# Two-layer hybrid encoder in float32: scheduling the state-space stage with shared and larger PSUM tiles, ScalarE order edges and sixteen filler projections

## Chip, cores and metric

The kernel runs on one core of a Trainium2 chip. The metric is the device time of one execution in microseconds. A TensorE weight load and the product that uses it are two instructions; the profile calls the first PEld and the second PE.

## The reference

A sequence of 1024 tokens of width 1024 goes through two layers, all in float32. Layer 0 multiplies by one wide matrix and splits the result: `z`, the state-space input `xbc` (x, B and C), `dt`, and four branches `Bg, Cg, h, gate` of a short convolution. Cut to what matters here:

```python
xbc = silu(depthwise_conv(xbc, conv_w) + conv_b)
cb = einsum('bclgn,bcsgn->bcgls', cq, bq)                      # C.B of a chunk of 128 tokens
y_diag = einsum('bcgls,bcgrls,bcsgrp->bclgrp', cb, segsum_exp(cs), xd)
states = einsum('bclgn,bcgrl,bclgrp->bcgrpn', bq, decay_states, xd)
y_off = einsum('bclgn,bcgrpn,bcgrl->bclgrp', cq, h_in, exp(cs))
y_a = rms_norm((y_diag + y_off) * silu(z))                     # both directions summed
y_b = sc_bg * depthwise_conv(sc_cg * sc_h) * silu(sc_gate)
x = layer_norm(alpha * x + concat([y_a, y_b]) @ w_out)
```

There are 4 groups of 4 heads and 8 chunks, in two directions. Layer 1 is an attention with rotary keys beside a pooling branch; its cosine and sine tables depend on the positions alone.

## The kernel before, in words

Every large product keeps float32 accuracy by splitting both operands into a high and a low part in the `fp32r` type (`split`, L492: a ScalarE cast, then a subtraction on VectorE or GpSimd) and adding three products (`mm3`, `mm6`).

Layer 0 (`layer0_main`, L501) goes in stages. First come `z` of group 0 and `dt`, accumulated in PSUM tiles `zdp` that `op_zx` (L568) empties. Then four branch tiles of 128 columns; each is a **filler**: 8 steps of `op_fm` (L678), 6 products a step, 48 products of 512 columns in a tile `gps`. Beside them `op_tp` (L853) loads x again, subtracts its quarters on VectorE and splits them into the four tiles `xT`, the right-hand sides of a Strassen scheme. `op_sw` and `op_sp` (L867, L923) then do two projection tiles as a **pair** in 84 products instead of 96: the eight pairs of B, C and x in front, and the pairs of the branches not yet done at the back.

Between the two lies the **state-space stage**, group by group. For each chunk `op_p2` (L721) transposes x and B (tile `xps`), multiplies by the decay (`xd` on VectorE) and splits it (`xdh` by a ScalarE cast, `xdl` on GpSimd); `op_p2s` (L741) multiplies to the chunk's state (`sps`), and the states are chained in `hin`. For groups 1 to 3 `op_z` (L701) computes that group's z in the same loop, 24 products of 256 columns in `zps`, with a tanh on ScalarE and a product on VectorE into the tile `zx`. Then, for each chunk, `op_p3f` (L780) multiplies C.B (`cbp`), loads a row of sums into all partitions (`E`, 512 KB), and makes the decay matrix: four biased copies on ScalarE (L794), a mask copied to PSUM (L795), a predicated copy on VectorE (L796), four exponentials (L798) and the product with C.B (L803). `op_p3b` (L808) adds the off-diagonal output `yo`, the diagonal output `yd` (four products with the decay matrix, L823) and the skip term, multiplies by z on GpSimd (L830) and squares on ScalarE (L831). `op_end` (L834) turns the sums of squares into `rinv`, which TensorE transposes (L841).

Fillers from a queue are laid between these steps by `main_plan` (L77): `FX` steps before group 0, `F2[g]` at each chunk of the first loop, `F3[g]` at each of the second. `J0` says how many branch columns of 128 are fillers; the rest are pairs. Within a plan step the Tile scheduler orders the instructions of each engine by its own timing, but it keeps an order that `tc.issue_after` gives: instructions of the block stand behind the one named, on that one's engine. `op_hold` (L674) uses this to keep fillers from being drawn ahead of a group's last transpose.

PSUM has two pools: `pa`, two tiles of 1024 columns (two banks each), and `pb`, four of one bank. Before, `gps` lies in `pa`; `xps`, `sps`, `zps`, `cbp`, `yo` and `yd` take turns in `pb`. The rotary tables (`rope_tables`, L351) are computed in group 2.

```python
F2, F3, FB, FX = (1, 0, 0, 0), (3, 2, 2, 3), 0, 8
JF, J0 = 1, 4
with tc.issue_after(st["xd", C2[E_AT]]):    # a VectorE instruction; L794 to L796 are in the block
```

Of the kernel before, what the change touches and what calls it, by code (L numbers as in the profile page):

```python
# [9 lines left out]
F32 = mybir.dt.float32  # L10
# [53 lines left out]
F2, F3, FB, FX = (1, 0, 0, 0), (3, 2, 2, 3), 0, 8  # L64
JF, J0 = 1, 4
# [3 lines left out]
ROPE_AT = (2, 2)  # L69
# [7 lines left out]
def main_plan():  # L77
# [41 lines left out]
    for g in range(G):  # L119
        ops.append(("z0", g))  # L120
        pull(FB)
        for i, c in enumerate(C2):
            ops.append(("p2", g, c))
            if g > 0:
                ops.append(("z", g, c))
            pull(F2[g])
            if (g, i) == ROPE_AT:
                ops.append(("rope",))
            if i > 0:
                ops.append(("p2s", g, C2[i - 1]))  # L130
# [15 lines left out]
        ops.append(("hold", None))  # L146
# [6 lines left out]
    pull(len(queue))  # L153
    ops.append(("sw", NF + 1, 0))
# [337 lines left out]
def split(nc, hi, lo, src, lo_eng, scale=None):  # L492
    if scale is None:
        nc.scalar.copy(out=hi, in_=src)  # L494
        lo_eng.tensor_tensor(out=lo, in0=src, in1=hi.bitcast(F32), op=ALU.subtract)  # L495
    else:
        nc.scalar.mul(out=hi, in_=src, mul=scale)
        nc.vector.scalar_tensor_tensor(out=lo, in0=src, scalar=scale, in1=hi.bitcast(F32), op0=ALU.mult, op1=ALU.subtract)


def layer0_main(k):  # L501
# [66 lines left out]
    def op_zx():  # L568
# [3 lines left out]
        for c, n, p in [(0, 2, zpair[0]), (2, 2, zpair[1])] + [(c, 1, zps[c].unsqueeze(1)) for c in range(4, NB)]:  # L572
# [4 lines left out]
            V.scalar_tensor_tensor(out=zs, in0=zt, scalar=1.0, in1=p[:, :, 0:256], op0=ALU.add, op1=ALU.mult)  # L577
# [55 lines left out]
    br = {}  # L633

# [39 lines left out]
    def op_hold(g):  # L674
        nonlocal hold
        hold = None if g is None else groups[g]["xp"]
# [24 lines left out]
    def op_z(g, c):  # L701
        st = groups[g]
        h, o = c // 4, (c % 4) * P
        ps = k.pb.tile([P, 512], F32, name="zps", tag="pb")[:, 0:256]
# [16 lines left out]
    def op_p2(g, c):  # L721
# [58 lines left out]
    def op_p3f(g, c):  # L780
# [11 lines left out]
        with tc.issue_after(st["xd", C2[E_AT]]):  # L792
# [58 lines left out]
    T = {}  # L851

    def op_tp(kk):  # L853
# [4 lines left out]
        for o, p, q in ((a0, a1, a0), (a1, b1, a1), (b1, b1, a0), (b0, b0, b1)):  # L858
            V.tensor_tensor(out=o, in0=p, in1=q, op=ALU.subtract)
# [763 lines left out]
```

## Time and profile before

| what | value |
|---|---|
| runs | 1483.84, 1486.55, 1487.31 us; median 1486.55 |
| profiled execution | 1484.99 us, its span 1483.2 us |
| granted TensorE clock, mean of the span | 0.968 |
| first stage, front pairs begin | 89.5 us |
| state-space stage, first transpose to last diagonal output | 253.8 to 601.6 us |
| first product of the back pairs | 617.7 us |
| back pairs end, output projection begins | about 773 us |

The span is the time from the first to the last instruction. An engine's busy time says how long it had an instruction in work, and not whether that ran at its best rate. The granted clock is TensorE's: 1 is 2.4 GHz, 0.5 is 1.2 GHz, and a value between is a mean over a stretch that had both.

### The profile page before, as it was taken

What the parts mean: (1) busy time and instruction counts of PE and PEld (TensorE: products, weight loads), DVE (VectorE), ACT (ScalarE), POOL (GpSimd) and SP (SyncE); (2) the same over time, 40 slices, a digit from 0 to 9 for tenths busy, and PEclk for the clock granted to TensorE, in tenths of its full rate; (3) what the DMA queues carried; (4) which work ended last, traced back from release to release, by engine and by line L of the source; (5) the groups of instructions that cost most, each with busy time, mean ns of one, the idle gap of its engine ahead of it and who ended that gap; (6) DMA issues with size and microseconds to landing.
All of it is one profiled execution on the core that took longest, in us unless ns stands there. A gap on an engine that the chain in (4) does not pass through costs nothing.

```text
span 1483.2 us, 19661 instructions
## 1 busy us (share of the span) xinstructions
PE 1394.1 (94%) x7191; PEld 1184.5 (80%) x7191; DVE 941.9 (64%) x1576; ACT 700.5 (47%) x1359; POOL 476.4 (32%) x459
## 2 busy tenths in 40 slices
PE   7999999697978899499999999999999999999997
PEld 7778888477867797388888888898888889888886
DVE  5758886364747558776656363643334888888575
ACT  4335554455554655343334342432223788888510
POOL 0022220353544545533320060242140255546311
PEclk9999999798989899799999999999999999999999
DMA  7412336544351613422236736311110000001232
GB/s 244 143 61 101 113 114 226 143 117 139 93 164 29 173 41 103 153 75 89 71 91 208 247 126 216 110 58 43 44 36 0 1 1 1 1 30 57 72 128 86
DMA packets 55520, 146.40 MB, mean 99 GB/s; under 512 B 6264, under 2 KB 11648, under 8 KB 55296
## 3 DMA queue, kind: packets, MB, share of 16 engines
q1 hardware_dynamic: 55424, 145.15, 31.4%
q8 instruction: 57, 0.93, 0.3%
q14 instruction: 39, 0.32, 0.1%
HBM read 118.78 MB, written 26.35 MB: 98 GB/s over the span
## 4 chain that ended last, share of the span: by engine, by line
PE 79%; DMA 7%; DVE 6%; ACT 3%; issue 3%; POOL 1%; SPq 0%; DVEq 0%; ACTq 0%; POOLq 0%
PE sA L939 12%; PE sD L939 6%; DMA E<-crow 5%; PE ops L423 4%; PE ops L425 4%; PE ops L422 4%; PE tps L1445 3%; PE fps L416 3%; PE sB L939 3%; PE fps L415 3%; PE fps L417 3%; PE gps L422 2%; PE gps L423 2%; PE sps L415 2%; PE gps L425 2%
## 5 line engine op out<-in xcount | busy, mean ns | idle before, releaser
L422 PE MATMUL gps<-x,whi 128*128 128x512 f32 x256 | 104.8, 409 | 6.3 <-DVE dtx L573 6.3
L1431 POOL TENSOR_SCALAR pt<-pt,sm 128x1024 f32<-128x1024 f32 x64 | 72.9, 1139 | 114.6 <-DVE sm L1430 63.8
L495 DVE TENSOR_TENSOR wlo<-wraw,whi 128x1024 fp32r<-128x1024 f32 x50 | 64.9, 1299 | 65.4 <-ACT whi L494 65.3
L423 PE MATMUL gps<-x,whi 128*128 128x512 f32 x256 | 104.8, 410 | 0.0
L888 POOL TENSOR_TENSOR s3t<-sraw 128x512 f32<-128x512 f32 x16 | 27.5, 1722 | 226.8 <-DMA sraw<-in_wt_dram 172.5
L494 ACT CAST whi<-wraw 128x1024 fp32r<-128x1024 f32 x50 | 52.3, 1049 | 94.7 <-PE ops L425 39.2
L495 DVE TENSOR_TENSOR PT<-tps,PT 128x512 fp32r<-128x512 f32 x128 | 84.2, 682 | 12.6 <-ACT PT L494 12.3
L425 PE MATMUL gps<-x,wlo 128*128 128x512 f32 x256 | 86.9, 410 | 0.0
L1425 DVE TENSOR_REDUCE nm<-sps 128x1 f32<-128x1024 f32 x64 | 78.0, 1218 | 9.2 <-PE sps L417 8.9
L1042 POOL TENSOR_TENSOR rs<-rs,neghalf 128x1 f32<-128x1 f32 x16 | 12.9, 810 | 210.5 <-DVE nm L1077 142.8
L1429 ACT ACTIVATE pt<-sps,nm 128x1024 f32<-128x1024 f32 x64 | 71.8, 1122 | 17.9 <-DVE nm L1426 15.2
L494 ACT CAST PT<-tps 128x512 fp32r<-128x512 f32 x128 | 70.0, 588 | 15.8 <-PE tps L1445 15.3
L495 POOL TENSOR_TENSOR xdl<-xd,xdh 128x512 fp32r<-128x512 f32 (+1 forms) x32 | 36.8, 1150 | 125.5 <-ACT xdh L494 115.9
L415 PE MATMUL fps<-x1hi,whi 128*128 128x512 f32 x192 | 74.9, 390 | 0.0
L417 PE MATMUL fps<-x1hi,wlo 128*128 128x512 f32 x192 | 74.7, 389 | 0.0
L416 PE MATMUL fps<-x1lo,whi 128*128 128x512 f32 x192 | 74.7, 389 | 0.0
L1445 PE MATMUL tps<-consts,pt 128*128 128x128 f32 x512 | 70.1, 272 | 0.5 <-DVE PT L495 0.5
L794 ACT ACTIVATE E<-E,ed 128x128 f32<-128x128 f32 x128 | 41.2, 390 | 57.4 <-DMA E<-crow 54.5
L629 DVE SCALAR_TENSOR_TENSOR cacc<-u,vec,cacc 128x1023 f32<-128x1023 f32 (+1 forms) x48 | 66.8, 1407 | 1.5 <-ACT cacc L626 1.3
L1460 PE MATMUL yps<-PT,vv 128*128 128x256 f32 x256 | 65.7, 286 | 0.0
L1445 PEld LDWEIGHTS tps<-consts,pt 128*128 128x128 f32 x512 | 59.7, 141 | 7.2 <-DVE PT L495 1.1
L494 ACT CAST whi<-sraw 128x1024 fp32r<-128x1024 f32 x40 | 41.2, 1049 | 50.4 <-PE sD L939 40.9
(381 smaller groups left out, 4357.7 us busy)
## 6 DMA issues: line engine op xcount, KB each, us to landing
wraw<-in_wt_dram SPq DMA_DIRECT2D x66, 512.0 KB, 4.4
sraw<-in_wt_dram SPq DMA_DIRECT2D x32, 512.0 KB, 3.6
E<-crow SPq DMA_DIRECT2D x32, 512.0 KB, 5.5
xtraw<-in_xT_dram SPq DMA_DIRECT2D x16, 512.0 KB, 4.3
xbd<-cacc SPq DMA_DIRECT2D x16, 512.0 KB, 2.6
xfm<-xbd SPq DMA_DIRECT2D x16, 512.0 KB, 6.8
ybd<-bra SPq DMA_DIRECT2D x16, 256.0 KB, 3.1
yad<-yg SPq DMA_DIRECT2D x32, 128.0 KB, 3.4
```

What stands on the lines that cost most here:

```text
L415: nc.tensor.matmul(out, shi, mhi, start=start, stop=False)
L416: nc.tensor.matmul(out, shi, mlo, start=False, stop=False)
L417: nc.tensor.matmul(out, slo, mhi, start=False, stop=stop)
L422: nc.tensor.matmul(out, shi, mhi, start=start, stop=False)
L423: nc.tensor.matmul(out, shi, mlo, start=False, stop=False)
L425: nc.tensor.matmul(out, slo, mhi, start=False, stop=stop)
L494: nc.scalar.copy(out=hi, in_=src)
L495: lo_eng.tensor_tensor(out=lo, in0=src, in1=hi.bitcast(F32), op=ALU.subtract)
L939: PE.matmul(ps, s_[:, kk, :], x_, start=fresh and kk == 0 and m == 0, stop=kk == 3 and m == 2, skip_group_check=True)
L1425: V.tensor_reduce(out=nm, in_=ps, axis=AX.X, op=ALU.max)
L1431: GP.tensor_scalar(out=pt, in0=pt, scalar1=sm, scalar2=1.0, op0=ALU.mult, op1=ALU.mult)
L1445: PE.transpose(out=ps[:, P * c:P * c + P], in_=pt[:, P * (4 * h + c):P * (4 * h + c) + P], identity=k.ident)
```

## The change

The diagonal output `yd` is put into the second half of the bank that held C.B (`cbp[:, 256:512]`), instead of a bank of its own. `zps` moves to the pool of large tiles. The biased copies and the mask copy of the decay matrix now stand behind the ScalarE cast `xdh` of the sixth chunk, where the edge before named a VectorE instruction. The subtractions of `op_tp` in front stand behind the last product of `op_zx` on VectorE. The rotary tables go to the output projection of layer 0, at its third weight. There are 16 fillers instead of 12 and six back pairs instead of eight; three fillers are held behind the last diagonal output.

```diff
-F2, F3, FB, FX = (1, 0, 0, 0), (3, 2, 2, 3), 0, 8
-JF, J0 = 1, 4
+F2, F3, FB, FX = (2, 0, 0, 0), (3, 3, 2, 2), 0, 8
+JF, J0 = 1, 5
...
-            if (g, i) == ROPE_AT:
-                ops.append(("rope",))
...
-        ops.append(("hold", None))
+        ops.append(("hold", None if g + 1 < G else "end"))
...
     pull(len(queue))
+    ops.append(("hold", None))
     ops.append(("sw", NF + 1, 0))
...
-            V.scalar_tensor_tensor(out=zs, in0=zt, scalar=1.0, in1=p[:, :, 0:256], op0=ALU.add, op1=ALU.mult)
+            T["after"] = V.scalar_tensor_tensor(out=zs, in0=zt, scalar=1.0, in1=p[:, :, 0:256], op0=ALU.add, op1=ALU.mult).ins
...
-        hold = None if g is None else groups[g]["xp"]
+        hold = None if g is None else groups[-1]["yd"] if g == "end" else groups[g]["xp"]
...
-        ps = k.pb.tile([P, 512], F32, name="zps", tag="pb")[:, 0:256]
+        ps = k.pa.tile([P, 1024], F32, name="zps", tag="pa")[:, 0:256]
...
-        split(nc, xh[:, cols], xl[:, cols], xd[:, cols], nc.gpsimd)
+        st["xa", c] = split(nc, xh[:, cols], xl[:, cols], xd[:, cols], nc.gpsimd)
...
-        with tc.issue_after(st["xd", C2[E_AT]]):
+        with tc.issue_after(st["xa", C2[E_AT]]):
...
-        st["f", c] = E
+        st["f", c] = E2[:, 0], cbp[:, 2 * P:4 * P]
...
-        yd = k.pb.tile([P, 512], F32, name="yd", tag="pb")[:, 0:256]
         for h in range(HPG):
-            PE.matmul(yd[:, HD * h:HD * h + HD], M[:, P * h:P * h + P], xt[:, HD * h:HD * h + HD], start=True, stop=True)
+            st["yd"] = PE.matmul(yd[:, HD * h:HD * h + HD], M[:, P * h:P * h + P], xt[:, HD * h:HD * h + HD], start=True, stop=True).ins
...
-        for o, p, q in ((a0, a1, a0), (a1, b1, a1), (b1, b1, a0), (b0, b0, b1)):
-            V.tensor_tensor(out=o, in0=p, in1=q, op=ALU.subtract)
+        with tc.issue_after(T["after"]) if "after" in T else nullcontext():
+            for o, p, q in ((a0, a1, a0), (a1, b1, a1), (b1, b1, a0), (b0, b0, b1)):
+                V.tensor_tensor(out=o, in0=p, in1=q, op=ALU.subtract)
...
+            if h == 0 and kk == ROPE_AT:
+                slots = [t[:, i] for t in (view(t4("rope"), 8) for _ in range(2)) for i in range(8)]
+                rope_tables(k, lambda name: slots.pop(0))
```

What the scheduler makes of it is shown at three places. The first is ScalarE in the first loop of group 0 (`xdh` the cast of a chunk's decayed x, `E` its biased copies, `zx`, `bhl` and `hin` copies out of PSUM). Before:

```order
145 L494 CAST xdh<-xd 128x256
146 L794 ACTIVATE E_2208<-E_2208,ed 128x128 x4
147 L641 ACTIVATE bra<-bru,vec 128x512 x2
148 L728 COPY zx<-xps 128x256
149 L494 CAST bhl<-xps 128x128
150 L794 ACTIVATE E_2227<-E_2227,ed 128x128 x4
151 L757 COPY hin<-sps 128x256
152 L494 CAST xdh<-xd 128x256
153 L794 ACTIVATE E_2289<-E_2289,ed 128x128 x4
154 L794 ACTIVATE E_2344<-E_2344,ed 128x128 x4
155 L494 CAST xdh<-xd 128x512
```

In the changed kernel, from the casts of the fifth and sixth chunk on:

```order
161 L493 CAST xdh<-xd 128x512 x2
162 L729 COPY zx<-xps 128x256
163 L493 CAST bhl<-xps 128x128
164 L795 ACTIVATE E_2265<-E_2265,ed 128x128 x4
165 L795 ACTIVATE E_2284<-E_2284,ed 128x128 x4
166 L795 ACTIVATE E_2345<-E_2345,ed 128x128 x4
167 L795 ACTIVATE E_2399<-E_2399,ed 128x128 x4
168 L493 CAST xdh<-xd 128x512
```

The biased copies of four chunks, which stood between the casts of the first three chunks, have moved behind the cast of the sixth.

The second place is TensorE from the end of group 0 to group 1 (`gps` a filler, `yo` and `yd` a chunk's outputs, `cbp` C.B, `xps` and `zps` transposes and z of group 1). Before:

```order
1105 L786 MATMUL cbp_2588<-xfm_1885 128x128
1106 L817 MATMUL yo_2625<-hin_1949,xfm_1885 128x256
1107 L823 MATMUL yd_2629<-zx_1947,E2_2518 128x64 x4
1108 L817 MATMUL yo_2662<-hin_1949,xfm_1885 128x256
1109 L823 MATMUL yd_2666<-zx_1947,E2_2590 128x64 x4
1110 L727 MATMUL xps_2693<-consts_63,xfm_2201 128x128 x3
1111 L415 MATMUL zps_2707<-whi_2551,x00_90 128x256
```

In the changed kernel (products on a `cbp` tile from L822 are diagonal outputs):

```order
1154 L822 MATMUL cbp_2522<-zx_1947,E2_2524 128x64 x4
1155 L424 MATMUL gps_2609<-x11_93,wlo_2439 128x512
1156 L414 MATMUL zps_2763<-whi_2603,x00_90 128x256
1157 L415 MATMUL zps_2763<-wlo_2604,x00_90 128x256
1158 L787 MATMUL cbp_2639<-xfm_1885 128x128
1159 L416 MATMUL zps_2763<-whi_2603,x00_90 128x256
1160 L414 MATMUL zps_2763<-whi_2603,x00_90 128x256
1161 L415 MATMUL zps_2763<-wlo_2604,x00_90 128x256
1162 L822 MATMUL cbp_2576<-zx_1947,E2_2578 128x64 x2
1163 L817 MATMUL yo_2676<-hin_1949,xfm_1885 128x256
```

Two tiles of z of the next group now lie between the last three diagonal outputs of the group, where nothing lay before.

The third place is TensorE at the end of the stage (`rinvp` the transpose of `rinv`, `sA` the first product of the back pairs). Before:

```order
2178 L425 MATMUL gps<-x_93,wlo 128x512
2179 L817 MATMUL yo<-hin,xfm 128x256
2180 L823 MATMUL yd<-zx,E_5187 128x64 x4
2181 L817 MATMUL yo<-hin,xfm 128x256
2182 L823 MATMUL yd<-zx,E_5245 128x64 x4
2183 L841 MATMUL rinvp<-consts,rinv 8x128
2184 L939 MATMUL sA<-x_90,whi 128x512 x2
```

In the changed kernel, around the same transpose:

```order
2286 L421 MATMUL gps<-x_90,whi 128x512
2287 L422 MATMUL gps<-x_90,whi 128x512
2288 L421 MATMUL gps<-x_92,whi 128x512
2289 L840 MATMUL rinvp<-consts,rinv 8x128
2290 L422 MATMUL gps<-x_92,whi 128x512
2291 L424 MATMUL gps<-x_90,wlo 128x512
```

Between the last diagonal output and that transpose there are now 57 filler products, and 39 more stand between it and the first product of the back pairs; the third held filler is laid into the first pair.

## Rows read from the trace of the kernel before

**Rows 1.** The page: busy time, share of the span and instructions of TensorE.

```profile
PE 1394.1 (94%) x7191; PEld 1184.5 (80%) x7191; DVE 941.9 (64%) x1576; ACT 700.5 (47%) x1359; POOL 476.4 (32%) x459
```

**Rows 2.** Stretch, length; busy PE, PEld, DVE, ACT, POOL; PEclk, DMA share, GB/s.

```profile
253.80:300.30 46.50, 33.78 (x145) 26.27 (x144) 19.29 (x32) 21.69 (x57) 13.17 (x15) 0.82 0.56 150
300.30:347.20 46.90, 39.10 (x194) 31.00 (x193) 30.03 (x69) 28.68 (x87) 27.56 (x36) 0.93 0.54 143
347.20:383.60 36.40, 36.35 (x259) 34.54 (x259) 15.09 (x35) 17.88 (x49) 14.63 (x16) 0.94 0.26 88
383.60:427.00 43.40, 37.16 (x176) 29.16 (x174) 31.93 (x70) 24.45 (x79) 23.31 (x35) 0.88 0.54 137
427.00:472.90 45.90, 39.88 (x260) 36.52 (x261) 27.55 (x78) 22.19 (x59) 15.50 (x17) 0.89 0.27 79
472.90:514.60 41.70, 36.66 (x175) 29.07 (x174) 28.31 (x64) 25.01 (x80) 25.17 (x35) 0.88 0.54 150
514.60:551.60 37.00, 36.65 (x260) 34.61 (x260) 15.15 (x35) 19.25 (x55) 16.20 (x19) 0.95 0.19 45
551.60:601.60 50.00, 45.48 (x223) 36.05 (x221) 43.03 (x84) 26.13 (x77) 25.31 (x32) 0.99 0.41 114
601.60:617.60 16.00, 0.03 (x1) 0.06 (x1) 11.45 (x15) 4.37 (x9) 11.25 (x10) 0.50 0.57 179
...
617.60:772.70 155.10, 155.10 (x694) 128.30 (x694) 99.19 (x105) 56.59 (x77) 48.36 (x32) 0.99 0.27 85
```

**Rows 3.** The chain that ended last, front pairs: start, duration, what.

```profile
150.04 2.73 PE sA L939 x12
...
169.19 2.73 PE sA L939 x12
```

**Rows 4.** Timeline of TensorE in group 0's second loop: start, duration, what.

```profile
320.92 1.02 PE L817 MATMUL yo<-hin,xfm 128*128 128x512 f32 x2
321.38 0.80 PE L422 MATMUL gps<-x,whi 128*128 128x512 f32 x1
...
322.72 1.00 PE L823 MATMUL yd<-zx,E 128*128 128x64 f32 x8
323.55 0.44 PE L786 MATMUL cbp<-xfm 128*128 128x128 f32 x2
323.75 0.48 PE L425 MATMUL gps<-x,wlo 128*128 128x512 f32 x1
```

**Rows 5.** Timeline of TensorE, two transposes of group 1, one chunk apart.

```profile
363.49 0.49 PE L727 MATMUL xps<-consts,xfm 128*128 128x128 f32 x3
...
367.38 0.49 PE L727 MATMUL xps<-consts,xfm 128*128 128x128 f32 x3
```

**Rows 6.** The chain that ended last, one product of z in group 1.

```profile
357.38 0.12 PE zps L416
```

**Rows 7.** What TensorE waited for from 250 to 620: total, times, longest.

```profile
PE sps L415 <- ACT xdh L494: 16.2, 5, 6.0
...
PE yd L823 <- DVE E L803: 3.2, 3, 1.6
```

**Rows 8.** Groups by line: ScalarE's biased copies, busy, mean ns, idle before and releaser.

```profile
L794 ACT ACTIVATE E<-E,ed 128x128 f32<-128x128 f32 x128 | 41.2, 390 | 57.4 <-DMA E<-crow 54.5 <-PE yd L823 3.0
```

**Rows 9.** Timeline of TensorE, diagonal outputs at the end of group 1.

```profile
421.22 1.94 PE L823 MATMUL yd<-zx,E 128*128 128x64 f32 x8 [2.92 <-issue]
...
425.23 1.97 PE L823 MATMUL yd<-zx,E 128*128 128x64 f32 x8 [1.11 <-DVE E L803]
```

**Rows 10.** Timeline of VectorE and TensorE in the first stage, before the first filler.

```profile
34.55 2.14 DVE L859 TENSOR_TENSOR xtraw<-xtraw 128x512 f32<-128x512 f32 x3 [1.43 <-DMA xtraw<-in_xT_dram]
...
39.34 0.68 DVE L577 SCALAR_TENSOR_TENSOR z<-zt,zdp 128x512 f32<-128x512 f32 x1
```

**Rows 11.** Timeline of TensorE in the first stage: last `zdp` product, first filler.

```profile
33.54 0.29 PE L417 MATMUL zdp<-zdh,x 128*128 128x288 f32 x1
40.17 0.77 PE L422 MATMUL gps<-x,whi 128*128 128x512 f32 x1 [6.33 <-DVE dtx L573]
```

More of the change, by code (lines that the diff above doesn't have):

```diff
@@ L68 @@
 E_AT = 5
-ROPE_AT = (2, 2)
+ROPE_AT = 2
 L1_ORDER = "t0 l2 t1 l3 t2 l4 t3 l5 m0 l6 m1 l7".split()
@@ L493, in split @@
     if scale is None:
-        nc.scalar.copy(out=hi, in_=src)
+        cast = nc.scalar.copy(out=hi, in_=src)
         lo_eng.tensor_tensor(out=lo, in0=src, in1=hi.bitcast(F32), op=ALU.subtract)
     else:
-        nc.scalar.mul(out=hi, in_=src, mul=scale)
+        cast = nc.scalar.mul(out=hi, in_=src, mul=scale)
         nc.vector.scalar_tensor_tensor(out=lo, in0=src, scalar=scale, in1=hi.bitcast(F32), op0=ALU.mult, op1=ALU.subtract)
+    return cast.ins
 def layer0_main(k):
@@ L633, in layer0_main @@
     br = {}
+    T = {}
     def br_conv(u, j):
@@ L735, in op_p2 @@
         d = dirs(cols)
-        st["xd", c] = V.tensor_tensor(out=xd.rearrange("p (q h d) -> p q h d", q=2, h=HPG)[:, d], in0=bc_mid(xv, 1, d.stop - d.start), in1=bc_last(dw4[:, c, d, g4], HD), op=ALU.mult).ins
+        V.tensor_tensor(out=xd.rearrange("p (q h d) -> p q h d", q=2, h=HPG)[:, d], in0=bc_mid(xv, 1, d.stop - d.start), in1=bc_last(dw4[:, c, d, g4], HD), op=ALU.mult)
         xh, xl = t2("xdh", F32R), t2("xdl", F32R)
-        split(nc, xh[:, cols], xl[:, cols], xd[:, cols], nc.gpsimd)
+        st["xa", c] = split(nc, xh[:, cols], xl[:, cols], xd[:, cols], nc.gpsimd)
         st["s", c] = (bh, bl, xh[:, cols], xl[:, cols])
@@ L804, in op_p3f @@
         st["cd", c] = cd[:, 0:4]
-        E = E2[:, 0]
-        st["f", c] = E
+        st["f", c] = E2[:, 0], cbp[:, 2 * P:4 * P]
     def op_p3b(g, c):
         st = groups[g]
-        M = st.pop(("f", c))
+        M, yd = st.pop(("f", c))
         g4 = slice(4 * g, 4 * g + 4)
@@ L849, in op_end @@
         nc.sync.dma_start(out=k.rrow, in_=rd.rearrange("c t -> (c t)").unsqueeze(0).partition_broadcast(P))
-    T = {}
     def op_tp(kk):
@@ L857, in op_tp @@
         a0, a1, b0, b1 = ra[:, 0:HALF], ra[:, HALF:S], rb[:, 0:HALF], rb[:, HALF:S]
-        for o, p, q in ((a0, a1, a0), (a1, b1, a1), (b1, b1, a0), (b0, b0, b1)):
-            V.tensor_tensor(out=o, in0=p, in1=q, op=ALU.subtract)
+        with tc.issue_after(T["after"]) if "after" in T else nullcontext():
+            for o, p, q in ((a0, a1, a0), (a1, b1, a1), (b1, b1, a0), (b0, b0, b1)):
+                V.tensor_tensor(out=o, in0=p, in1=q, op=ALU.subtract)
+        if kk == 3:
+            T.pop("after", None)
         t = big(k, "xT4").rearrange("p (s a t) -> p s a t", s=2, a=4)
@@ L1015, in op_ya @@
         split(nc, t[:, 0, :, o:o + P], t[:, 1, :, o:o + P], view(y, KD), V)
-    table = {"fm": op_fm, "hold": op_hold, "zx": op_zx, "ssd": op_ssd, "xl": op_xl, "z0": op_z0, "z": op_z, "p2": op_p2, "p2s": op_p2s, "p2b": op_p2b, "p3f": op_p3f, "p3b": op_p3b, "dt": op_dt, "rope": lambda: rope_tables(k, t2), "end": op_end, "ya": op_ya, "tp": op_tp, "sw": op_sw, "sp": op_sp}
+    table = {"fm": op_fm, "hold": op_hold, "zx": op_zx, "ssd": op_ssd, "xl": op_xl, "z0": op_z0, "z": op_z, "p2": op_p2, "p2s": op_p2s, "p2b": op_p2b, "p3f": op_p3f, "p3b": op_p3b, "dt": op_dt, "end": op_end, "ya": op_ya, "tp": op_tp, "sw": op_sw, "sp": op_sp}
     for op in main_plan():
```

## The prediction

> **What bounds the kernel now.** The page comes first: TensorE is busy 1394.1 of 1483.2 us, and no other engine is busy for more than two thirds of the span [rows 1]. So time can be won only where TensorE stands still or runs slowly, or by giving it fewer products. The table by stretch says where [rows 2]: in the back pairs it is busy all the time at a clock of 0.99, while in the 363.8 us from the first transpose of the state-space stage to the back pairs it is busy 305.1 and the clock is as low as 0.82.
>
> Busy is not the whole story there, since a product that runs at half clock or waits inside its slot counts as busy. So I count what each stretch would need at the pace of the trace's good places. A filler product takes 2.73 / 12 = 0.227 us [rows 3], a filler of 48 products 10.9. A chunk of the second loop takes 0.46 for `yo`, 0.83 for `yd` and 0.20 for C.B, 1.49 in all, by the starts that follow one another [rows 4]. A chunk of the first loop with z takes 367.38 - 363.49 = 3.89 [rows 5]; z alone is 24 x 0.12 = 2.9 [rows 6], so a chunk of group 0, without z, takes about 1.0. The number of filler products in each stretch is read from TensorE's order.
>
> - Group 0, first loop: 46.5 less (96 x 0.227 + 8 x 1.0 = 29.8): **16.7 lost**. Second loop: 46.9 less (96 x 0.227 + 8 x 1.49 = 33.7): **13.2**.
> - Group 1: 36.4 less (16 x 0.227 + 8 x 3.89 = 34.7): **1.7**; 43.4 less (80 x 0.227 + 11.9 = 30.1): **13.3**.
> - Group 2: 45.9 less 34.7: **11.2**; 41.7 less 30.1: **11.6**.
> - Group 3: 37.0 less 34.7: **2.3**; 50.0 less (128 x 0.227 + 11.9 = 41.0): **9.0**.
> - End, last `yd` to the back pairs: **16.0**.
>
> That is 95.0 us, of which the busy column shows 58.7 as idle. The waits say what the largest are: 16.2 us for the cast `xdh` [rows 7], 16.0 at the end where TensorE is busy for 0.03 [rows 2]. ScalarE itself stood idle for 54.5 us before its biased copies, waiting for `E` to land [rows 8]; its queue is in order, so the casts behind those copies waited too.
>
> **The change part by part.** *Order edges on ScalarE.* In group 0 the copies of four chunks stood between the casts of the first three; now they stand behind the sixth. Most of TensorE's 16.2 us for casts lay there (five waits, the longest 6.0 [rows 7]). With two filler steps a chunk instead of one the loop also has cover for the 16 copies (16 x 41.2 / 128 = 5.1 us [rows 8]) that now precede the last two casts. Bounds for what stays lost: 2 (as in group 1's first loop) and 16.7. I take 4, nearer to group 1, since the order has 30 filler products, 6.8 us, right beside those copies.
>
> *Rotary tables.* They go out of group 2's first loop, which then resembles groups 1 and 3 (1.7 and 2.3 lost): 2 instead of 11.2. VectorE was busy 27.6 us there and 15.1 in group 1's first loop [rows 2], so some 12 us go. In the output projection the order lays them singly between the weight splits, and VectorE is busy 64% over the span [rows 1]; so I cost them at 1 us, with bounds 0 and 5. The cover is the next weight, split one step ahead; if it goes, TensorE waits for that weight.
>
> *z in large tiles, shared bank.* In the tails of the second loops nothing lay between the last outputs, and TensorE went cold: `yd` took 1.94 there [rows 9] and 1.00 beside fillers [rows 4], and two outputs lay 425.23 - 421.22 = 4.0 us apart, 2.5 more than their work. Now two z of the next group, 5.8 us, lie there in groups 0 to 2. They are not new work, only earlier. But the tile `zx` that they are written to is free only when GpSimd has read the last chunk, and `pa` has two slots; so the third z waits for last `yd`, sum, product and evacuation, about 3 us, and with the cold clock after it I put 4 at each of the three boundaries (bounds 0 and 6). What is queued behind that z on TensorE are the transposes and states of group 1 to 3, so all of it is on the path.
>
> *Fillers.* Group 0 and 1 have 3 steps for each chunk, 4.1 us beside 1.49, more than the 4.0 of an unfilled chunk: 6 and 5 stay lost. Group 2 has 2, and its order has four outputs behind the last z: 4 x 2.5 = 10 if nothing had run ahead; I take 9. Group 3 has 2 where it had 3, five outputs without filler or z (5 x 2.5 = 12.5), and VectorE there still has the quarters of x to split (it was busy 43.0 of 50.0 [rows 2]): 14 instead of 9.0. At the end 57 products, 12.9 us, lie ahead of `rinvp`, which came 16.0 after the last output: about 2 stays, slow clock included. In sum the losses kept are 4 + 6 + (2 + 4) + 5 + (2 + 4) + 9 + (2 + 4) + 14 + 2 = 58 of 95: **37 won**. The work itself grows: four fillers, 43.6, against two pairs of 169.19 - 150.04 = 19.15 [rows 3], 38.3: **5.3 lost**.
>
> *First stage.* The first filler started at 40.17 after a gap of 6.33 [rows 11], because VectorE had subtractions and splits of x ahead of the product that frees the tile; that product ran at 39.34 for 0.68 [rows 10]. Behind the edge the gap needs the addition, a tanh and that product, an estimate of 1.7 us; and without the long gap the first products don't run cold. I take **5 won**, bounds 0 and 6. What is queued behind on VectorE is the split of x and, through its three raw buffers on SP's queue, the first pair's weights. They have room: the front pairs start only after four fillers, 43.6 us.
>
> Sum: 37 - 5.3 + 5 - 1 = 35.7 us. The profiled execution took 1484.99, so 1449.3, and I say **1449**; the median of the runs shown is 1486.55, 1.6 above that execution. With the bounds at their good ends (30 us kept) it would be 1419, with the bad ones (87 kept, nothing won in front, 5 lost on the tables) 1487.
>
> **The rivals.** *Everything fills.* If with more chunks in flight the decay chain runs ahead, the tails of groups 2 and 3 shrink with the others. For it: ScalarE no longer waits for `E` in line, and a chunk's copies take it 41.2 / 32 = 1.3 us [rows 8], far under 4.0. Against it: VectorE's load in group 3. With 35 kept: 60 - 5.3 + 5 = 59.7, **1425**.
>
> *The chunk's pace stays.* C.B now holds its bank until the diagonal output has been read. If that ties the next chunk as much as a third bank did, the second loops lose what they lost before (13.2, 13.3, 11.6) and group 3 some 18 with five bare chunks; with 4 + 6 + 6 + 6 for the first loops and 2 at the end that is 80 kept: 15 - 5.3 + 5 - 1 = 13.7, **1471**. For it: pace 4.0 in a tail that had all engines free. Against it: `yd` already waited for the last reading of C.B (3.2 us in three waits [rows 7]), so the sharing adds no wait of its own. The Trainium skill speaks on its side: Perfetto Trace Analysis, under Matmuls, wants independent groups of products to rotate through different PSUM banks so that emptying one overlaps the next; by that rule this change would cost what this rival costs, and no run here shows the shared bank yet.
>
> *A wait takes the place of the one removed (slower).* The biased copies now stand in the first loops, where z has only two slots. If `E` lands later than the sixth cast, ScalarE waits with the tanh of z, the last casts and copies behind it, and TensorE stops within two chunks. The wait that ScalarE had was 54.5 us [rows 8]. If all of it reached TensorE, 35.7 - 54.5 = -18.8, **1504**; it decides from 35.7 of the 54.5 on. Against it: the loads of `E` stand in SP's queue as early as before, and the copies come three chunks later.
>
> *The edge in front doesn't help.* The tiles of x come late, and the first pair waits as long as the filler did: 5 lost instead of won, **1459**.
>
> **How the numbers follow.** Forecast 0.60, everything fills 0.14, pace stays 0.14, the edge in front 0.07, slower 0.05. The forecast's own range is 1435 to 1465; to hold 8 in 10 it reaches to the first rival and to the second's edge: **1424 to 1470**. A change of 0.3%, 4.5 us, is about what a measurement can tell from none. Only the slower rival and the worst bounds of the second come near that line: faster 0.92, same 0.03, slower 0.05.
>
> **What would show it.** Right: no wait of TensorE for `xdh` above 2 us in group 0; first filler near 35.5 us; group 2's first loop near 38; two z between the last outputs with a gap of some 3 us behind them; gaps and a low clock left in the tails of groups 2 and 3; `rinvp` with a wait under 4. Wrong: gaps on TensorE for tanh or `xdh` behind the copies, outputs still 4 us apart beside fillers, waits for a weight while the rotary tables run, or front pairs that begin no earlier than 89 us.

## The result, and the profile after

The changed kernel takes 1450.68 us (median of 4 runs, 1448.25 to 1452.92), the kernel before beside it 1486.93 (1483.84 to 1488.05): a ratio of 0.976, 95% interval 0.974 to 0.978, 36 us less. The forecast was 1449. The profiled execution has a span of 1448.4 us against 1483.2, so 34.8 us less; the sum had come to 35.7. That nearness is partly luck: the term for the first stage was wrong by more than its size, and the stage made it good, as the stretches show.

The page of the changed kernel: busy time, share of the span and instructions of TensorE. TensorE is busy as long as before, in a shorter span [rows 1].

```profile
PE 1393.8 (96%) x7215; PEld 1184.6 (82%) x7215; DVE 925.5 (64%) x1564; ACT 693.6 (48%) x1350; POOL 464.8 (32%) x452
```

The same nine stretches as in [rows 2], now each second loop ending with the group's last diagonal output; the last one ends with the first product of the back pairs.

```profile
254.20:297.70 43.50, 40.86 (x189) 33.30 (x188) 22.03 (x35) 22.62 (x58) 13.31 (x15) 0.96 0.60 173
297.70:342.80 45.10, 44.99 (x251) 37.37 (x250) 34.13 (x72) 26.27 (x76) 25.72 (x34) 1.00 0.56 139
342.80:378.10 35.30, 31.92 (x216) 29.89 (x215) 15.96 (x34) 20.41 (x62) 16.12 (x19) 0.90 0.40 120
378.10:426.60 48.50, 48.50 (x266) 40.39 (x265) 30.40 (x69) 25.53 (x78) 27.40 (x38) 1.00 0.47 140
426.60:459.10 32.50, 31.70 (x223) 29.24 (x223) 14.58 (x33) 19.55 (x58) 15.55 (x16) 1.00 0.35 118
459.10:502.60 43.50, 39.97 (x214) 32.99 (x213) 30.75 (x71) 22.86 (x71) 21.75 (x31) 0.91 0.47 123
502.60:541.20 38.60, 32.74 (x215) 30.54 (x214) 16.52 (x34) 20.48 (x60) 16.30 (x18) 0.84 0.18 51
541.20:584.60 43.40, 37.77 (x169) 28.01 (x168) 35.17 (x75) 24.69 (x75) 27.55 (x34) 0.88 0.44 115
584.60:609.30 24.70, 22.21 (x98) 17.71 (x97) 17.77 (x23) 8.91 (x15) 8.03 (x8) 1.00 0.46 143
```

With the unit costs of the prediction and the products that TensorE's order has in each stretch, the losses can be set beside the ones it expected to stay. For group 0's first loop, for example, 135 filler products make 30.6 and eight chunks 8.0, so 43.5 - 38.6 = 4.9 are lost. Products of z that now run in the loop before are counted where they run.

| stretch | lost before | predicted to stay | lost after |
|---|---|---|---|
| group 0, first / second loop | 16.7 / 13.2 | 4 / 6 | 4.9 / 3.2 |
| group 1 | 1.7 / 13.3 | 6 / 5 | 5.5 / 2.8 |
| group 2 | 11.2 / 11.6 | 6 / 9 | 1.1 / 9.7 |
| group 3 | 2.3 / 9.0 | 6 / 14 | 8.8 / 14.5 |
| end | 16.0 | 2 | 2.7 |
| sum | 95.0 | 58 | 53.2 |

So 41.8 us came out of this stage's losses instead of 37. What TensorE still waits for there (its waits from 250 to 622 us: total, times, longest) is mostly the tile `zx` at the three group boundaries, which before did not show; the casts, 16.2 before [rows 7], are down to 2.6.

```profile
PE zps L414 <- DVE zx L711: 9.9, 3, 5.9
PE cbp L787 <- DVE to L820: 3.8, 2, 3.0
PE yo L817 <- DVE to L820: 3.6, 2, 2.6
PE sps L414 <- ACT xdh L493: 2.6, 1, 2.6
```

The three waits for `zx` are 3.4, 0.7 and 5.9 us. The trace names what stands behind the longest: `zx` is written at 508.66, when GpSimd has finished its last product `yg` (507.93 to 508.65). The sum which that product reads was ready at 506.20, and GpSimd then waited for the landing of an earlier `yg` (the DMA `yad<-yg`). So some 1.7 of the 5.9 us are a store and not the chain of the last chunk; no run tried more buffers for `yg`.

ScalarE's own idle time before the biased copies fell from 54.5 us [rows 8] to 23.8:

```profile
L795 ACT ACTIVATE E<-E,ed 128x128 f32<-128x128 f32 x128 | 40.1, 390 | 25.4 <-DMA E<-crow 23.8 <-PE cbp L822 1.6
```

The tail of group 0, TensorE's timeline (start, duration, what; idle time and its releaser in brackets). Products of z now run between the last outputs; the third z waits 3.38 us for `zx` and then takes some 0.21 us a product where 0.12 is usual.

```profile
335.13 0.55 PE L822 MATMUL cbp<-zx,E 128*128 128x64 f32 x4
335.50 0.36 PE L416 MATMUL zps<-whi,x 128*128 128x256 f32 x1
...
338.69 0.60 PE L817 MATMUL yo<-hin,xfm 128*128 128x256 f32 x2
...
341.74 1.10 PE L822 MATMUL cbp<-zx,E 128*128 128x64 f32 x8
...
346.56 0.58 PE L414 MATMUL zps<-whi,x 128*128 128x256 f32 x1 [3.38 <-DVE zx L711]
346.94 0.42 PE L415 MATMUL zps<-wlo,x 128*128 128x256 f32 x1
347.15 0.42 PE L416 MATMUL zps<-whi,x 128*128 128x256 f32 x1
```

The first stage won nothing. The first filler starts at 34.05 instead of 40.17 [rows 11] and the fillers end 8 us earlier, but TensorE then waits for `cs`, the copy of the decay sums. Before:

```profile
88.73 1.05 PE L487 MATMUL rps<-consts,cs 128*32 128x128 f32 x8 [2.03 <-ACT cs L471]
89.53 0.71 PE L939 MATMUL sA<-x,whi 128*128 128x512 f32 x2
```

In the changed kernel:

```profile
77.66 0.38 PE L462 MATMUL cps<-dtmp,consts 128*128 128x128 f32 x2
...
86.64 1.89 PE L486 MATMUL rps<-consts,cs 128*32 128x128 f32 x8 [7.93 <-ACT cs L470]
88.18 1.20 PE L939 MATMUL sA<-x,whi 128*128 128x512 f32 x2
```

On ScalarE that copy stands behind three casts for the pairs, and the first two of them waited 3.24 and 0.72 us for GpSimd's additions. A table load and an activation of a branch stand between them too:

```profile
81.09 0.62 ACT L493 CAST s<-s3t 128x512 fp32r<-128x512 f32 x1 [3.24 <-POOL s3t L888]
82.42 1.05 ACT L493 CAST whi<-sraw 128x1024 fp32r<-128x1024 f32 x1 [0.72 <-POOL sraw L893]
83.49 1.28 ACT L666 ACT_TABLE_LOAD   x1
84.78 0.60 ACT L666 ACTIVATE brt<-gps 128x512 f32<-128x512 f32 x1
85.28 1.04 ACT L493 CAST whi<-sraw 128x1024 fp32r<-128x1024 f32 x1
86.21 0.38 ACT L470 COPY cs<-cps 128x256 f32<-128x256 f32 x1
```

The front pairs begin at 88.18 instead of 89.53, and their first 12 products run at a mean clock of 0.59 (the second tile `sB` starts 4.6 us after the pairs begin, before 2.8), so the state-space stage begins at 254.2 where it began at 253.8.

### The profile page after: what moved, and what is told of

It is laid out like the page before. It is cut to its first block, busy times and chain, and to the rows that moved or that the text cites. A ratio compares the mean times of both kernels' runs of the same rounds, so it can differ in the third digit from the quotient of the medians.

```text
span 1448.4 us, 19638 instructions
## 1 busy us (share of the span) xinstructions
PE 1393.8 (96%) x7215; PEld 1184.6 (82%) x7215; DVE 925.5 (64%) x1564; ACT 693.6 (48%) x1350; POOL 464.8 (32%) x452
## 4 chain that ended last, share of the span: by engine, by line
PE 79%; DMA 8%; DVE 8%; ACT 2%; issue 2%; POOL 1%; SPq 0%; DVEq 0%; ACTq 0%; POOLq 0%
PE sA L939 11%; PE sD L939 5%; PE ops L421 4%; PE ops L424 4%; PE ops L422 4%; PE tps L1448 3%; PE fps L416 3%; PE fps L414 3%; PE fps L415 3%; PE gps L421 3%; PE gps L422 3%; PE gps L424 3%; PE sB L939 3%; PE sps L414 2%; PE sps L415 2%; PE sps L416 2%
## 5 line engine op out<-in xcount | busy, mean ns | idle before, releaser
L422 PE MATMUL gps<-x,whi 128*128 128x512 f32 x320 | 127.4, 398 | 0.0
L421 PE MATMUL gps<-x,whi 128*128 128x512 f32 x320 | 126.4, 395 | 0.1
L494 DVE TENSOR_TENSOR wlo<-wraw,whi 128x1024 fp32r<-128x1024 f32 x54 | 72.5, 1342 | 58.5 <-ACT whi L493 58.4
L493 ACT CAST whi<-wraw 128x1024 fp32r<-128x1024 f32 x54 | 56.7, 1050 | 102.3 <-PE ops L424 41.3
L424 PE MATMUL gps<-x,wlo 128*128 128x512 f32 x320 | 103.4, 401 | 0.0
L888 POOL TENSOR_TENSOR s3t<-sraw 128x512 f32<-128x512 f32 x14 | 23.1, 1653 | 235.0 <-DMA sraw<-in_wt_dram 197.5
L424 PEld LDWEIGHTS gps<-x,wlo 128*128 128x128 f32 x320 | 59.8, 188 | 15.6 <-issue 3.6
L421 PEld LDWEIGHTS gps<-x,whi 128*128 128x128 f32 x320 | 60.3, 188 | 13.1 <-issue 0.7
L422 PEld LDWEIGHTS gps<-x,whi 128*128 128x128 f32 x320 | 60.2, 188 | 12.7 <-issue 1.0
L414 PE MATMUL zps<-whi,x 128*128 128x256 f32 x192 | 58.2, 303 | 10.0 <-DVE zx L711 9.9
```

The costliest lines, as they stand in the source:

```text
L414: nc.tensor.matmul(out, shi, mhi, start=start, stop=False)
L421: nc.tensor.matmul(out, shi, mhi, start=start, stop=False)
L422: nc.tensor.matmul(out, shi, mlo, start=False, stop=False)
L424: nc.tensor.matmul(out, slo, mhi, start=False, stop=stop)
L493: cast = nc.scalar.copy(out=hi, in_=src)
```

## The experiments

Each run left a trace, and all are read in the same way: the stage, from the first transpose to the first product of the back pairs, less its work (149.3 us for chunks and z, within 0.3 of 8 x 1.0 + 24 x 3.89 + 32 x 1.49 by the prediction's unit costs, and 10.9 for each filler in it) is what it loses. Ratios are to the kernel before, measured beside each; the changed kernel's is 0.976. A hundredth of a ratio is 14.9 us. Two ratios are called different here if they are over some 0.003 apart, an estimate from the widths of the intervals.

| kernel | ratio (95%) | front pairs | stage | fillers in it | lost |
|---|---|---|---|---|---|
| before | 1 | 89.5 | 363.9 | 11 | 94.7 |
| changed | 0.976 (0.974-0.978) | 88.2 | 355.1 | 14 | 53.2 |
| no edge in front | 0.979 (0.977-0.981) | 88.4 | 361.5 | 14 | 59.6 |
| edge at the first z | 0.975 (0.972-0.978) | 89.0 | 354.6 | 14 | 52.7 |
| group 2, three steps | 0.968 (0.966-0.970) | 87.9 | 357.1 | 15 | 44.3 |
| group 3, three steps | 0.971 (0.969-0.973) | 88.2 | 360.1 | 15 | 47.3 |
| VectorE edge | 0.981 (0.978-0.984) | 89.2 | 365.0 | 14 | 63.1 |
| rotary in group 2 | 0.985 (0.983-0.987) | 88.5 | 366.5 | 14 | 64.6 |
| both banks as before | 0.979 (0.976-0.981) | 88.1 | 362.8 | 14 | 60.9 |
| twelve fillers | 0.991 (0.989-0.994) | 88.4 | 353.1 | 11 | 83.9 |
| output in its own bank | 0.974 (0.972-0.976) | 87.9 | 355.6 | 14 | 53.7 |
| z in small banks | 0.982 (0.980-0.984) | 88.0 | 365.6 | 14 | 63.7 |
| decay sums later | 0.984 (0.982-0.986) | 77.8 | 363.8 | 15 | 51.0 |
| and second quarter later | 0.984 (0.982-0.986) | 78.3 | 361.1 | 15 | 48.3 |

### The first stage

```diff
-        with tc.issue_after(T["after"]) if "after" in T else nullcontext():
+        with nullcontext():
```

> The changed kernel without the order edge on the subtractions of x in the first stage. Theory: the edge only moves a wait. The three raw buffers carry x and then the first pair's weights, so with the edge x is split later, the weights land later, and the 5.9 us that the fillers begin earlier are waited for again before the front pairs. Then without it the first filler starts near 40, behind a gap of some 6 us, the front pairs start between 87 and 90 us, and the time is within 3 us of the changed kernel's 1450.7. Rival, the prediction's term: the edge is worth 5 us, so 1455 to 1457 without it.

Median 1456.84. TensorE's timeline of this run shows the front as the theory had it: the gap before the first filler is back, and the pairs begin where they began with the edge, at full clock after a gap of only 2 us.

```profile
39.48 0.76 PE L421 MATMUL gps<-x,whi 128*128 128x512 f32 x1 [4.74 <-DVE dtx L573]
...
87.62 1.05 PE L486 MATMUL rps<-consts,cs 128*32 128x128 f32 x8 [2.03 <-ACT cs L470]
```

The stage begins at 252.7, 1.5 us earlier than with the edge. So the edge wins nothing in front. The total is nevertheless 4.5 us higher (0.979 to 0.976), at the edge of what can be told and more than the theory allowed. The rival's number came out, and not at the rival's place; the table says where: 6.4 more are lost in the stage. Its order has 31 filler products in group 1's first loop where the changed kernel has 21, and TensorE waits 6.4 us for the casts instead of 2.6. The scheduler laid out groups 1 to 3 differently; why an edge in front brings that about was not tried, so what the 4.5 us owe to the edge stays open.

```diff
-            T["after"] = V.scalar_tensor_tensor(out=zs, in0=zt, scalar=1.0, in1=p[:, :, 0:256], op0=ALU.add, op1=ALU.mult).ins
+            T.setdefault("after", V.scalar_tensor_tensor(out=zs, in0=zt, scalar=1.0, in1=p[:, :, 0:256], op0=ALU.add, op1=ALU.mult).ins)
```

> The edge in front names the first product of z on VectorE (at 33.2 us in the changed kernel) instead of the last (at 40.8, behind stores of z). Theory (raw buffers bound the first stage): the first subtraction of x comes at 34 to 36 us instead of 41.5, the last at 68 to 70 instead of 75.9, the first filler stays near 34, the front pairs begin at 82 to 84 instead of 88.2 and at full clock, and the time is 5 to 8 us less than the changed kernel's: 1443 to 1446. Rival (the loads themselves, one queue for all, are what comes late): pairs at 86 to 88, 1449 to 1452. Second rival (only the cast of the decay sums on ScalarE, queued behind weight casts, is late): pairs at 86 to 88 as well, with the wait for that copy kept at 6 to 8 us.

Median 1449.90, the same as the changed kernel. Here the first theory falls. The subtractions begin at 33.96 as expected, 7.5 us earlier (the last comes at 72.4 instead of 75.9), and yet the pairs begin at 89.04. TensorE's timeline shows that the wait has only changed its name: it is on the chain of the decay sums on VectorE and then on ScalarE.

```profile
83.74 0.80 PE L462 MATMUL cps<-dtmp,consts 128*128 128x128 f32 x2 [5.77 <-DVE dtmp L456]
...
87.50 1.89 PE L486 MATMUL rps<-consts,cs 128*32 128x128 f32 x8 [1.69 <-ACT cs L470]
89.04 1.20 PE L939 MATMUL sA<-x,whi 128*128 128x512 f32 x2
```

The second rival comes nearest, since it names the decay sums; but the greater wait is a step earlier than it said, for VectorE's `dtmp` (5.77), and that for the copy is 1.69 where it expected 6 to 8. The next test takes that step away from in front of the pairs (it also has the three steps of group 2, below, and is read against that kernel):

```diff
-    ops.append(("dt",))
-    pairs(0, NF, SW_FRONT, {})
+    pairs(0, NF, SW_FRONT, {0: [("dt",)]})
```

> The kernel with three filler steps in group 2, and besides the step that makes the decay sums (their transposes stood ahead of the first front pair on TensorE) moved behind the first pair. Theory: what kept the front pairs from starting when the fillers ended was the copy of these sums, queued on ScalarE behind two casts of weights; so sA starts at 78 to 80 us, right behind the last filler product, some 3 to 5 us of waits for split weights show inside the first pair, and the time is 3 to 6 us below the 1440.3 of the kernel without the move: 1434 to 1437. Rival (the split weights of the first pair are as late as the copy): the second product tile of the pair starts no earlier than 91 us and the time is 1438 to 1442.

Median 1463.32, 0.016 above the kernel without the move, some 24 us slower. The first half of the expectation holds: the pairs begin at 77.83, right behind the last filler product, and wait only 1.10 and 0.68 us inside the first pair. So the decay sums had kept them, and the weights had not, or by no more than these 1.8 us. But the step holds the VectorE work that makes `dtmp` as well, and that had run beside the fillers; moved as a whole it stands on VectorE behind weight splits and convolutions of the pairs (its first instruction runs at 109.4), and TensorE meets the transposes with nothing ready:

```profile
120.41 0.80 PE L461 MATMUL cps<-dtmp,consts 128*128 128x128 f32 x2 [20.88 <-DVE dtmp L455]
```

The 10 us won in front are lost twice over: the state-space stage begins at 269.4 instead of 253.8, 6.7 more are lost in it, and 3.1 behind it. Moving the transposes without the VectorE steps was not tried.

### The tails of the second loops

```diff
-F2, F3, FB, FX = (2, 0, 0, 0), (3, 3, 2, 2), 0, 8
+F2, F3, FB, FX = (2, 0, 0, 0), (3, 3, 3, 2), 0, 8
```

> Three filler steps a chunk in group 2's second loop instead of two; one of the three held fillers, the one that lay in the first back pair, goes there. Theory: the tail of that loop lost 9.7 us for lack of cover, as group 0 and 1 with three steps lose 3.3 and 2.7; so the 10.9 us of the filler come for 4 to 6 and the time is 1443 to 1447. Rival: the tail is set by the decay chain of the last chunks whatever lies before it, so the filler only lengthens the stretch by what it saves at the back: 1449 to 1452.

Median 1440.31, 0.008 or 12 us below the changed kernel and better than either theory. Group 2's second loop in the stretch table:

```profile
459.20:506.70 47.50, 47.50 (x263) 39.60 (x262) 33.88 (x75) 25.08 (x75) 25.78 (x33) 1.00 0.47 129
```

TensorE has no idle time and a clock of 1.00 there, where it had 0.91. The filler lengthens the stretch by 4 us instead of 10.9, and the loss falls from 9.7 to 2.7. Group 3's first loop and the end lose another 5 less, and its tail 3 more. The back pairs and all behind them take 12.6 us less without the filler that stood there. This is the fastest of all kernels that were run.

```diff
-F2, F3, FB, FX = (2, 0, 0, 0), (3, 3, 2, 2), 0, 8
+F2, F3, FB, FX = (2, 0, 0, 0), (3, 3, 2, 3), 0, 8
```

> The same filler into group 3's second loop, which lost 14.4 us in the changed kernel. Theory (cover is short): the loss falls to 6 to 9 and the time is 1442 to 1446. Rival (VectorE, busy 35.1 of 43.3 us there with the quarters of x, sets the tail): the loss stays at 13 or more and the time is 1449 to 1452.

Median 1443.90, 7 us below the changed kernel. The time is the theory's, but the loss is neither side's: the loop grows to 51.8 us, its loss falls only from 14.5 to 12.0, and the clock stays under 1. The filler lengthens the whole stage by 5.0 us, and the back pairs and all behind them take 12.3 less without it.

```profile
539.60:591.40 51.80, 44.65 (x216) 35.50 (x216) 42.35 (x82) 28.19 (x82) 33.72 (x37) 0.96 0.41 111
```

So in group 3 short cover alone does not set the tail. In the changed kernel the two halves of that loop look like this (stretches as above): VectorE, the third pair of numbers, is busy for 21.0 of the first 21.8 us, and in the second half TensorE idles at a low clock.

```profile
541.20:563.00 21.80, 21.80 (x104) 17.52 (x103) 20.97 (x38) 9.97 (x27) 14.98 (x15) 1.00 0.60 154
563.00:584.60 21.60, 15.97 (x66) 10.49 (x65) 14.21 (x37) 14.71 (x50) 12.57 (x20) 0.76 0.28 76
```

TensorE's waits in that second half come to 5.5 us, and VectorE's instructions release all of them (the longest, 2.6, ends with the product that empties `yo`). But VectorE itself is busy for only 14.2 of the 21.6 us there, so in that half it is not short of time.

On top of the kernel with the later decay sums, the second quarter of x was put behind the last output:

```diff
-            if g == G - 1 and i == NB - 1:
-                ops.append(("tp", 1))
...
+    ops.append(("tp", 1))
     ops.append(("tp", 2))
```

> As the run before, and besides the second quarter of x is subtracted and split behind the last output instead of in the last chunks of group 3. Theory: in the first half of group 3's second loop VectorE was busy for 21.0 of 21.8 us, so the chunks fell behind while the fillers ran out, and 5.6 us of idle time at a clock of 0.76 followed in the second half; without some 4 us of the quarter there the loop is 2 to 4 us shorter and the time 1 to 3 us less than the run before. Rival (the three quarters behind the last output now come late for the back pairs): the end, from the last output to the back pairs, grows by 3 us or more and the time is the same or higher.

Median 1462.23, no different from the run before (1463.32). The trace tells why this decides nothing: the loop takes 44.9 us against 45.2, and VectorE's timeline still has the same subtractions of x in its first half: the scheduler drew them there from the new place too.

```profile
564.10:586.50 22.40, 21.80 (x106) 17.14 (x104) 17.97 (x34) 9.32 (x28) 14.26 (x15) 1.00 0.52 130
```

Whether VectorE's load sets group 3's tail stays open.

### The banks

```diff
-        ps = k.pa.tile([P, 1024], F32, name="zps", tag="pa")[:, 0:256]
+        ps = k.pb.tile([P, 512], F32, name="zps", tag="pb")[:, 0:256]
...
-        st["f", c] = E2[:, 0], cbp[:, 2 * P:4 * P]
+        st["f", c] = E2[:, 0]
...
+        yd = k.pb.tile([P, 512], F32, name="yd", tag="pb")[:, 0:256]
```

> The changed kernel with z and the diagonal output both in single banks of their own, as before. Theory: by the order no z lies in the tails of the second loops any more, so groups 0 to 2 lose 4 to 6 us each more there, against 10 us of waits for zx at the group boundaries that go: net 5 to 12 more, 1456 to 1463. Rival (the Trainium skill's rule on rotating banks, in Perfetto Trace Analysis under Matmuls): the outputs of a chunk overlap better in banks of their own, and the time is 3 to 10 less: 1441 to 1448.

Median 1456.33, 0.979 against 0.976: some 4 us more than the changed kernel, at the theory's low end and barely to be told. To tell the two edits apart each was undone alone. The output in its own bank (the last two hunks):

> The changed kernel with the diagonal output alone back in a bank of its own; z stays in the large tiles. Theory: by the order z still lies in the tails (36, 16 and 48 products instead of 48, 42 and 48), but a chunk then takes three turns of the four small banks instead of two, so fewer chunks are in flight and the tails are longer: 2 to 6 us more than the changed kernel, 1452 to 1457. Rival (the Trainium skill's rule on rotating banks, in Perfetto Trace Analysis under Matmuls): the next C.B no longer waits for the reading of the output, and the time is 3 to 8 less: 1443 to 1448.

Median 1448.69: 0.974 against 0.976, no difference. Both sides miss. The stage loses 53.7 instead of 53.2. So with z in the large tiles sharing the bank costs nothing that can be told and gives nothing; it did not buy the further chunks in flight that I expected of it. The rule in the Trainium skill (Perfetto Trace Analysis, Matmuls) that independent groups of products should rotate through different banks makes no measurable difference at this place. A chunk's C.B and its diagonal output are not independent, though, since the output's weights are made from C.B. The other edit alone, z in the small banks:

> The changed kernel with z alone back in the small banks; C.B and the diagonal output share one. Theory: by the order 24, 23 and no products of z are left in the tails where 48, 42 and 48 lay, so some 3, 2 and 6 us of cover go, against part of the 9.9 us of waits for zx that go too: 1450 to 1456. Rival (the sharing is what pays, and z gains nothing where it lies): within 2 us of the changed kernel, 1449 to 1452.

Median 1460.24, 0.982 against 0.976: 9 us, and above the range expected. The four second loops lose 9.5, 5.4, 16.3 and 19.1, in sum 20 more than in the changed kernel; the first loops of groups 1 to 3, without waits for `zx`, lose 9.5 less. The last two second loops, as stretches, show the clock falling:

```profile
462.90:508.40 45.50, 37.93 (x174) 29.15 (x173) 33.40 (x73) 22.92 (x74) 25.69 (x33) 0.88 0.48 135
546.00:594.30 48.30, 43.02 (x173) 32.02 (x173) 38.25 (x77) 25.52 (x76) 27.88 (x34) 0.77 0.44 123
```

Group 3's tail suffers too, though no z follows it; there the order has the same outputs and 76 filler products instead of 75, so cover is not all of it. What else differs there was not looked for.

This run and the one with both banks as before differ in the bank of the output alone. With z in the small banks the bank of its own gives 0.979 and the shared one 0.982, some 5 us, just over what can be told. So sharing shows no gain in either layout, and with z in the small banks it may cost a little. The gain of the two edits is z's move: 6 to 7 us with the output in its own bank (0.974 against 0.979), 9 with the shared one.

### ScalarE's edge, the rotary tables, the fillers

```diff
-        with tc.issue_after(st["xa", C2[E_AT]]):
+        with tc.issue_after(st["xd", C2[E_AT]]):
```

> The changed kernel with the order edge of the biased copies back on the VectorE product of the sixth chunk, so that ScalarE's order is free again. Theory: ScalarE's copies slip in front of the casts of the first chunks as before, TensorE waits 8 to 16 us for the cast xdh in group 0's first loop, and the time is 8 to 13 us more than the changed kernel's: 1459 to 1464. Rival: two filler steps a chunk cover the late casts by themselves: 1449 to 1454, with less than 4 us of waits for xdh.

Median 1459.40: 0.981 against 0.976, 7 us by the ratios and 9 by the medians, at the low end of the range. Group 0's first loop grows by 4.5 us (48.1 for 43.6) with six filler products fewer in it, so it loses some 6 more; but the waits for `xdh` in the stage grow only from 2.6 to 5.9:

```profile
PE sps L414 <- ACT xdh L493: 5.9, 2, 4.3
```

So the cover of two filler steps a chunk does part of what the edge was credited with, as the rival had it; of the 9.9 us that the stage loses more, some 6 lie in that loop and 6 in groups 1 and 2, and group 3 loses less.

```diff
-ROPE_AT = 2
+ROPE_AT = (2, 2)
...
+            if (g, i) == ROPE_AT:
+                ops.append(("rope",))
...
```

> The changed kernel with the rotary tables back in the first loop of group 2. Theory: they add some 12 us of VectorE's time to a stretch of 32.2 us and lengthen it by 6 to 10, while the output projection gains the 1.9 us by which it is longer than before: 1455 to 1459. Rival: z in the large tiles lets TensorE run past VectorE's delay, and the tables cost nothing in either place: 1448 to 1452.

Median 1466.42: 0.985, 14 us, more than expected. Group 2's first loop takes 45.8 us instead of 32.5, with VectorE (third number pair) busy for 26.3 instead of 14.6 and TensorE's clock down to 0.89; behind the first back product another 4.0 are lost.

```profile
424.70:470.50 45.80, 37.31 (x225) 32.95 (x225) 26.32 (x76) 22.91 (x62) 14.25 (x16) 0.89 0.25 84
```

In the output projection they cost nothing that can be seen: from the first back pair to the end the three-step kernels, with the tables there, take 826.5 and 826.8 us, and the kernel before, without them, 865.5 - 38.3 for its two further pairs = 827.2.

```diff
-F2, F3, FB, FX = (2, 0, 0, 0), (3, 3, 2, 2), 0, 8
-JF, J0 = 1, 5
+F2, F3, FB, FX = (1, 0, 0, 0), (3, 2, 2, 3), 0, 8
+JF, J0 = 1, 4
```

> The changed kernel with twelve fillers and eight back pairs, spread over the groups as before, and so none held behind the last output. Theory: the end shows again a gap of 14 to 16 us before the transpose of rinv, where the changed kernel loses 2.7, the second loops of groups 1 lose some 5 more, and the work of two pairs for four fillers is 5.3 less: 1458 to 1464. Rival (fillers merely fill what would shrink by itself): 1444 to 1450.

Median 1474.96: 0.991 against 0.976, 23 us, well over the range. The gap at the end is back in TensorE's waits,

```profile
PE zps L414 <- DVE zx L711: 19.8, 3, 8.1
PE rinvp L840 <- DVE rinv L838: 10.8, 1, 10.8
```

at 10.8 and not 14 to 16, and beside it the waits for `zx` are twice those of the changed kernel. What I had not counted is how little the fillers in the stage cost: with three fewer in it the stage is only 2.0 us shorter (353.1 to 355.1). Those three, 32.7 us of work, were laid almost wholly into holes. And with all other edits in place twelve fillers give 13 of the 36 us; the step to sixteen gives the other 23. The run takes three things back together, the four fillers, the second step a chunk in group 0 and the three fillers held at the end; they were not told apart.

## Why the prediction was right, and where it was not

- **The losses of the stage: right.** 53.2 us stay where 58 were predicted, and the single stretches are within 3 us but for group 2's first loop (1.1 for 6). The three boundaries cost 3.4, 0.7 and 5.9 us of waits where 4 each was put down: the mechanism (the third z waits for `zx`) was right, and the sizes scatter, with a store of `yg` in the longest that the term did not have. At the end 2.7 us stay for 2.
- **The edge in front: wrong.** The step that failed is "I take 5 won", with its ground that what is queued behind has "room: the front pairs start only after four fillers". The gap before the first filler did close, and the first filler came at 34.05 where 35.5 was named. But the pairs began 1.35 us earlier instead of 6, and the lower clock behind the longer gap took that back: 0.4 lost. The split of x and the weights had nearly that room (1.8 us of waits in the run with the decay sums later). What had none were the decay sums, which the term leaves out. Their transposes stand on TensorE between the fillers and the pairs, and they already waited 2.0 us for a copy on ScalarE in the trace of before. The sign named for this failure, pairs no earlier than 89 us, was drawn too tight: they began at 88.18 and nothing was won. The rival for it (1459, with 0.07) was right that the wait only moves. It blamed late tiles of x, against which the run with the edge at the first z speaks (x subtracted up to 7.5 us earlier, the pairs no earlier), and had 5 lost for 0.4.
- **The two errors cancelled.** 41.8 won in the stage, less 5.3 for the fillers' work, 0.4 lost in front, 1.0 lost behind the first back product (839.1 us for 865.5 - 38.3 + 10.9 = 838.1) and 0.3 of rounding in the unit costs, give 34.8, as measured. The 4.8 us more in the stage come from group 2's first loop (4.9 better than predicted) and the second loops of groups 0 and 1 (5.0 better), less group 3's first loop (2.8 worse) and small ones.
- **What each part is worth.** The prediction credited group 0's first loop mostly to the edge on ScalarE; the run without that edge loses some 6 us there, and the run with one filler step a chunk about 5 (39.8 us with 96 products and eight chunks, 10.0 lost for 4.9). The rotary tables' move was right in kind, 9 predicted in that loop and 13 found, and the 1 us for the output projection does not show in the three-step kernels. The parts do not add up: taken back one at a time, fillers, rotary tables, z, ScalarE's edge and the edge in front cost 23, 14, 9, 7 and 4 us, in sum more than the 36 of the whole, so each is what it is worth with the others in place.
- **The rival of the shared bank** did not come about: the bank of its own gives the same time, and the second loops lose 3.2, 2.8 and 9.7 where it had 13.2, 13.3 and 11.6. The rival that ends slower neither: ScalarE's wait for `E` fell by 30.7 us and no wait of TensorE took its place there.
- **Group 3's tail** was sized rightly (14.5 for 14). The reason given, VectorE's quarters of x, is neither shown nor refuted, and that the size fits is so far luck.
- **Other signs.** TensorE waited 2.6 us for `xdh` in group 0, where at most 2 was named, and group 2's first loop took 32.5 us, not near 38. The third z behind a gap, the low clock in the tails of groups 2 and 3 (0.91 and 0.88) and a wait of `rinvp` under 4 (1.6) came as named.

## What to carry to other kernels

A filler's cost is its work less the hole that it fills. Busy time does not tell the holes, since a product at half clock counts as busy; a table of stretches at the pace of full cover does. Before an edit that ends a wait is given its worth, list what stands next on the engine that waited, and whose queue releases that: here the next instructions already had a short wait, which took over nearly all that was won. And when a step is moved, move the part that is late, not the part that feeds it.

## What had not been expected of the hardware

A wait that moves takes its low clock along. Without the edge in front TensorE waited 2.0 us ahead of the front pairs and their first products ran at a granted clock of 1.00, the 2.4 GHz level:

```profile
88.40:91.20 2.80, 2.80 (x15) 2.33 (x13) 2.80 (x4) 1.80 (x4) 2.17 (x2) 1.00 0.56 195
```

In the changed kernel, after 7.9 us of waiting, the same products ran at a mean of 0.59, most of it at the 1.2 GHz level, and those behind them at 1.00:

```profile
88.20:92.70 4.50, 4.50 (x14) 3.61 (x13) 3.62 (x6) 1.08 (x3) 3.73 (x3) 0.59 0.70 195
92.70:97.80 5.10, 5.10 (x23) 4.15 (x23) 1.90 (x2) 1.64 (x2) 0.27 (x1) 1.00 0.18 64
```

The first row of these two holds the changed kernel's first twelve products of the front pairs, the second those that follow. By the starts of the second tile the lower clock cost 4.6 - 2.8 = 1.8 us beside the gap itself, more than the 1.35 us by which the pairs began earlier.

It is no accident of one trace. In the ten runs in which TensorE waited 6.4 us or more in all ahead of the pairs, the second tile starts 3.5 to 4.8 us after the first; in the four in which it waited 2.0 us or not at all (before, no edge in front, and the two with the decay sums later), 2.7 to 2.9.

Nor is it a new loss. In the kernel before, the same low clock stood ahead of the fillers: behind the gap of 6.33 us [rows 11] their first 4.5 us ran at 0.55, and all four took 45.7 us. In the changed kernel they begin at 1.00 and take 43.8. The edge won 6.1 us of waiting and 1.9 us of slow clock at the first filler, and the front pairs paid back both.
